# Four rows per ScalarE and VectorE instruction, and a last tile stored in two pieces, in a streaming GELU-gate kernel

## The chip, the cores and the metric

The kernel runs on one core of one Trainium2 chip. The metric is the device time of an execution in microseconds (us), lower is better. The profile is one execution taken by the hardware profiler; its span is about 1.8 us shorter than the device time. Engines: ACT is ScalarE, DVE is VectorE, SP is SyncE (here it only issues DMAs); 16 DMA engines move data between HBM (the chip's large memory) and SBUF (the core's own memory).

## The reference, cut to what matters

```python
x = randn(32, 512, 2048)                      # float32
x1, x2 = x[..., :1024], x[..., 1024:]
out = 0.5 * x1 * (1 + erf(x1 / sqrt(2))) * x2 # float32, (32, 512, 1024)
```

134.22 MB are read and 67.11 MB written. There is no reuse.

## The kernel before

There are 16384 rows of 2048 numbers. A tile holds 8 rows in each of the 128 partitions, so there are 16 tiles: 8.4 MB to load and 4.2 MB to store for each. Two input buffers and two output buffers rotate.

```python
xpool = ctx.enter_context(tc.tile_pool(name="xpool", bufs=2))
opool = ctx.enter_context(tc.tile_pool(name="opool", bufs=2))
# load(i): one dma_start on the SP queue, 8.4 MB
ahead = [load(0), load(1)]
for i in range(n_tiles):
    x_tile = ahead.pop(0)
    o_tile = opool.tile([P, R, half], out.dtype, name="o_tile")
    last = i == n_tiles - 1
    pieces = 4 if last else 1
    step = R // pieces
    for k in range(pieces):
        for r in range(k * step, (k + 1) * step):
            nc.scalar.activation(
                out=x_tile[:, r, :half], in_=x_tile[:, r, :half], func=GELU)
            nc.vector.tensor_mul(
                out=o_tile[:, r, :], in0=x_tile[:, r, :half], in1=x_tile[:, r, half:])
        rows = slice(k * step, (k + 1) * step)
        queue = nc.sync if i >= n_tiles - 2 else nc.scalar
        queue.dma_start(out=o_t[i][:, rows, :], in_=o_tile[:, rows, :])
    if i + 2 < n_tiles:
        ahead.append(load(i + 2))
# ... (cut: flattening, launch)
```

Stores of tiles 0 to 13 go on ACT's queue. The last two go on SP's queue, so tile 14's store stands in line behind the last load there.

Of the kernel before, what the change touches and what calls it, by code (L numbers as in the profile page):

```python
# [1 line left out]

# [4 lines left out]

GELU = mybir.ActivationFunctionType.Gelu


@with_exitstack
def kernel(
    ctx: ExitStack,
    tc: tile.TileContext,
    x: bass.AP,
    out: bass.AP,
):





    nc = tc.nc
    P = nc.NUM_PARTITIONS

    x_flat = x.flatten_outer_dims()
    out_flat = out.flatten_outer_dims()
    n_rows, dim = x_flat.shape
    half = dim // 2

    R = 8
    x_t = x_flat.rearrange("(n p r) d -> n p r d", p=P, r=R)
    o_t = out_flat.rearrange("(n p r) d -> n p r d", p=P, r=R)
    n_tiles = x_t.shape[0]

    xpool = ctx.enter_context(tc.tile_pool(name="xpool", bufs=2))
    opool = ctx.enter_context(tc.tile_pool(name="opool", bufs=2))

    def load(i):
        x_tile = xpool.tile([P, R, dim], x.dtype, name="x_tile")  # L40
        nc.sync.dma_start(out=x_tile, in_=x_t[i])  # L41
        return x_tile

    ahead = [load(0), load(1)]
    for i in range(n_tiles):
        x_tile = ahead.pop(0)
        o_tile = opool.tile([P, R, half], out.dtype, name="o_tile")
        last = i == n_tiles - 1
        pieces = 4 if last else 1
        step = R // pieces  # L50
        for k in range(pieces):
            for r in range(k * step, (k + 1) * step):
                nc.scalar.activation(  # L53
                    out=x_tile[:, r, :half], in_=x_tile[:, r, :half], func=GELU
                )
                nc.vector.tensor_mul(  # L56
                    out=o_tile[:, r, :],
                    in0=x_tile[:, r, :half],
                    in1=x_tile[:, r, half:],
                )  # L60
            rows = slice(k * step, (k + 1) * step)
            queue = nc.sync if i >= n_tiles - 2 else nc.scalar
            queue.dma_start(out=o_t[i][:, rows, :], in_=o_tile[:, rows, :])
        if i + 2 < n_tiles:
            ahead.append(load(i + 2))


# [1 line left out]
_INS = ['x']  # L69
_OUTS = [((32, 512, 1024), 'float32')]  # L70


# [23 lines left out]
```

## Time and profile before

The median was 472.28 us (472.03 to 472.85, 3 runs). What matters:

| reading | value | view |
|---|---|---|
| DMA while in steady state | 433 to 434 GB/s | windows |
| ACT busy, DVE busy | 26%, 31% | page |
| a tile lands every | 29.0 us | landings in the trace |
| compute of a tile, landing to last product | 10.3 us | timeline |
| last load lands | 450.05 us | chain of waits |
| span | 470.5 us | page |

These are lines of the page of the kernel before: busy time of the engines, DMA in 40 slices of the span (9 means 90% or more), the queue of kind "instruction", the chain that ended last, and the two costly groups (line, engine, operation, tiles, shapes, count, then busy us and mean ns of one, then idle time before them).

```profile
DVE 146.7 (31%) x128; ACT 124.2 (26%) x129; POOL 0.2 (0%) x4
...
DMA  8999999999999999999999999999999999999987
...
q14 instruction: 2, 0.02, 0.0%
HBM read 134.22 MB, written 67.11 MB: 428 GB/s over the span
...
DMA x_tile<-in_x_dram 80%; DVE o_tile L56 15%; ACT x_tile L53 2%; DVEq L91 0%; SPq L41 0%; ACTq L53 0%
...
L56 DVE TENSOR_TENSOR o_tile<-x_tile 128x1024 f32<-128x1024 f32 x128 | 146.7, 1218 | 313.7 <-ACT x_tile L53 313.7
L53 ACT ACTIVATE x_tile<-x_tile 128x1024 f32<-128x1024 f32 x128 | 122.9, 1042 | 332.9 <-DMA x_tile<-in_x_dram 332.9
```

The DMA row is full from end to end; both compute engines mostly wait. The chain gives DVE 15%, but that isn't 15% to gain: it follows one of two buffers, and while that buffer is computed on, the other buffer's load is moving.

This is the chain of waits of the kernel before in order of time (start us, length us, what).

```profile
115.36 47.63 DMA x_tile<-in_x_dram
...
173.36 48.46 DMA x_tile<-in_x_dram
...
232.20 47.59 DMA x_tile<-in_x_dram
...
406.07 43.98 DMA x_tile<-in_x_dram
450.05 0.02 issue
...
450.14 1.07 ACT x_tile L53
...
451.23 6.90 DVE o_tile L56 x6
```

### The profile page before, as it was taken

Reading aid. Unit: us, or ns where it says so; the run is one execution under the profiler, and the core shown is the slowest. Engines: PE = TensorE matmul, PEld = TensorE weight load, DVE = VectorE, ACT = ScalarE, POOL = GpSimd, SP = SyncE. Lnnn points to the kernel's source line nnn. Section 1 sums busy time; section 2 is a strip of 40 time slices with the busy share of each in tenths; the row PEclk is TensorE's granted clock in tenths of the full one; section 3 lists DMA queues with packets and bytes.
Section 4 is the critical chain, followed back from the end, with each engine's and each line's share of the span. In section 5 each row is a group of like instructions: output and inputs, shape, how many; then the busy total and the mean of one; then the engine's idle time right before and its main releaser. Section 6 shows DMA issues by size and latency. Waiting matters only on the chain.

```text
span 470.5 us, 408 instructions
## 1 busy us (share of the span) xinstructions
DVE 146.7 (31%) x128; ACT 124.2 (26%) x129; POOL 0.2 (0%) x4
## 2 busy tenths in 40 slices
DVE  0070704307052070520705216061150702507061
ACT  1050605105060150601506024060230603306060
POOL 0000000000000000000000000000000000000000
DMA  8999999999999999999999999999999999999987
GB/s 357 446 446 373 457 423 418 468 429 418 418 446 429 446 407 469 424 429 412 460 432 435 426 443 429 415 437 457 418 443 418 454 440 423 423 449 412 471 382 337
DMA packets 5042, 201.35 MB, mean 428 GB/s; under 512 B 560, under 2 KB 560, under 8 KB 560
## 3 DMA queue, kind: packets, MB, share of 16 engines
q1 hardware_dynamic: 3024, 142.61, 70.4%
q10 hardware_dynamic: 2016, 58.72, 28.9%
q14 instruction: 2, 0.02, 0.0%
HBM read 134.22 MB, written 67.11 MB: 428 GB/s over the span
## 4 chain that ended last, share of the span: by engine, by line
DMA 80%; DVE 15%; ACT 2%; DVEq 0%; issue 0%; SPq 0%; ACTq 0%
DMA x_tile<-in_x_dram 80%; DVE o_tile L56 15%; ACT x_tile L53 2%; DVEq L91 0%; SPq L41 0%; ACTq L53 0%
## 5 line engine op out<-in xcount | busy, mean ns | idle before, releaser
L56 DVE TENSOR_TENSOR o_tile<-x_tile 128x1024 f32<-128x1024 f32 x128 | 146.7, 1218 | 313.7 <-ACT x_tile L53 313.7
L53 ACT ACTIVATE x_tile<-x_tile 128x1024 f32<-128x1024 f32 x128 | 122.9, 1042 | 332.9 <-DMA x_tile<-in_x_dram 332.9
L53 ACT ACT_TABLE_LOAD x1 | 1.3, 1283 | 0.7 <-PEq L80 0.7
L80 POOL MEMSET const-uint8-127<- 128x1 uint8 x1 | 0.1, 102 | 0.0
L80 POOL MEMSET const-bfloat16-1.0<- 128x1 bf16 x1 | 0.1, 101 | 0.0
L80 POOL MEMSET const-float32-0.0<- 128x1 f32 x1 | 0.1, 98 | 0.2 <-issue 0.2
L80 POOL MEMSET const-float32-1.0<- 128x1 f32 x1 | 0.1, 98 | 0.0
## 6 DMA issues: line engine op xcount, KB each, us to landing
out_dram<-o_tile ACTq DMA_DIRECT2D x14, 4096.0 KB, 37.9
out_dram<-o_tile SPq DMA_DIRECT2D x1, 4096.0 KB, 24.7
out_dram<-o_tile SPq DMA_DIRECT2D x4, 1024.0 KB, 8.9
x_tile<-in_x_dram SPq DMA_DIRECT2D x16, 47.6
```

The source lines that it names most:

```text
L53: nc.scalar.activation(out=x_tile[:, r, :half], in_=x_tile[:, r, :half], func=GELU)
L56: nc.vector.tensor_mul(out=o_tile[:, r, :], in0=x_tile[:, r, :half], in1=x_tile[:, r, half:],)
L80: nc = _bacc.Bacc("TRN2", target_bir_lowering=False, num_devices=1)
```

## The change

The intent: fewer, larger instructions, so that their fixed cost is paid a quarter as often (128 products and 128 GELUs become 32 and 32). The last tile has two steps, and each is stored when done.

```diff
-    R = 8
+    R, STEP = 8, 4
...
-        pieces = 4 if last else 1
-        step = R // pieces
-        for k in range(pieces):
-            for r in range(k * step, (k + 1) * step):
-                nc.scalar.activation(
-                    out=x_tile[:, r, :half], in_=x_tile[:, r, :half], func=GELU
-                )
-                nc.vector.tensor_mul(
-                    out=o_tile[:, r, :],
-                    in0=x_tile[:, r, :half],
-                    in1=x_tile[:, r, half:],
-                )
-            rows = slice(k * step, (k + 1) * step)
-            queue = nc.sync if i >= n_tiles - 2 else nc.scalar
-            queue.dma_start(out=o_t[i][:, rows, :], in_=o_tile[:, rows, :])
+        for r in range(0, R, STEP):
+            rows = slice(r, r + STEP)
+            nc.scalar.activation(
+                out=x_tile[:, rows, :half], in_=x_tile[:, rows, :half], func=GELU
+            )
+            nc.vector.tensor_mul(
+                out=o_tile[:, rows, :],
+                in0=x_tile[:, rows, :half],
+                in1=x_tile[:, rows, half:],
+            )
+            if last:
+                store(nc.sync, i, o_tile, rows)
+        if not last:
+            store(nc.sync if i == n_tiles - 2 else nc.scalar, i, o_tile, slice(0, R))
```

More of the change, by code (lines that the diff above doesn't have):

```diff
@@ L42, in load, with store @@
         return x_tile
+    def store(queue, i, o_tile, rows):
+        queue.dma_start(out=o_t[i][:, rows, :], in_=o_tile[:, rows, :])
     ahead = [load(0), load(1)]
```

## The prediction

> **What bounds the kernel now.** The 16 DMA engines. The page has DVE 31% and ACT 26% busy, DMA digits of 9 from end to end, 201.35 MB moved. The windows view reads 433 to 434 GB/s in each 58 us stretch between 106 and 396 us; the DMA packets in the trace keep a share of 1.0 until about 468 us. DVE and ACT only wait (waits view: ACT 332.9 us for loads, DVE 313.7 us for ACT). The Trainium skill ("SBUF — State Buffer", the DMA setup-cost knee) gives 436 GB/s as the port-side asymptote of 16 DMA engines; this trace agrees with 433.
>
> The chain of waits says "DMA 80%, DVE 15%", alternating a load of 47.6 us with 10.26 us of compute. That 15% is misleading: one buffer's load waits for DVE to free it, but the other buffer's load is then in flight. A tile lands every 29.0 us, so the next load is issued 10.3 us into a 29 us stretch in which the queue still has work. About 18 us of slack.
>
> **What the change does.** Elements and bytes stay the same. One row: ACT lasts 1.040 us, pitch 0.949; DVE lasts 1.217, pitch 1.136 (timeline: 7.68 and 9.17 us for eight). With 1024 elements at the slopes these imply (about 0.833 ns and 1.042 ns an element), the fixed cost is about 96 ns of pitch on ACT and 69 ns on DVE. The Trainium skill ("Perfetto Trace Analysis", Optimizing Scalar/DVE Operations) states about 93 and 60 ns; agrees. Estimates for four rows: ACT lasts 3.60 (pitch 3.51), DVE lasts 4.42 (pitch 4.34). Busy: DVE 146.7 -> about 140, ACT 124.2 -> about 115. None of that saving is on the critical path.
>
> Coarser pieces cost latency: DVE now starts after 3.60 us of ACT instead of 1.04. From landing to the last product: 3.60 + 0.03 + 4.34 + 4.42 = 12.4 us against 10.3: +2.1 us a tile. In the 15 first tiles slack absorbs it: each load is issued 2.1 us later and lands at the same time (issue to landing 47.6 -> about 45.5 us). The chain will show about DMA 76, DVE 14, ACT 6%, over the same span.
>
> **Only the end counts.** The last load lands at 450.05 us. Tile 14's store, queued behind it, keeps the DMA engines full until 458.0 to 458.5 us. Before, the first quarter of the last store is issued at 453.6 us, so no gap: data flow until 468.3 us, the last piece lands at 469.5 and the span ends at 470.5. After, the first half is issued at about 450.14 + 3.60 + 0.03 + 4.42 + 0.1 = 458.3 us, just when the engines run dry. With about 1 us from issue to first packet (first load: issued 0.73, first packets after 1.5) the engines idle about 1 us. The second half is issued 4.34 us later, less than the 4.84 us that 2.1 MB take at 433 GB/s, so no second gap. Larger packets (the 8 KB ones run at 428 GB/s) return 0.1 us. Net +0.9 us: predicted 473.2 us, 472.1 to 474.8.
>
> **What would show it.** Right: loads land every 29.0 us; 433 GB/s in the middle; DVE near 140 us; last load landing within 0.5 us of 450; a dip of DMA share near 458 to 460 us; last data near 469. Wrong: a middle period other than 29.0 us; no dip; last load landing elsewhere.
>
> **What would make it wrong.** A larger start delay for a store on an empty ring (2 us would give +1.9); loads and stores interleaving differently once issued 2 us later; four-row instructions costing more than the sum of rows because of their jump between rows; chip-to-chip differences. A change over 2% (9.4 us) would need the middle to lose its overlap, 0.6 us per tile.

## The result, and the profile after

The changed kernel took 471.48 us (471.29 to 472.08, 6 runs), the kernel before 472.22 us (472.03 to 472.85, 6 runs). The ratio is 0.9985, with a 95% interval of 0.9972 to 0.9998. Ratios here are the mean time of one kernel's runs over that of the other's of the same rounds, so not quite the ratio of the medians quoted. By the rule of 2% this is the same time. I had said 472.1 to 474.8 us: a little slower. It was a little faster, outside the range.

The lines of the page after that answer to those of before:

```profile
DVE 140.2 (30%) x32; ACT 115.2 (25%) x33; POOL 0.2 (0%) x4
...
DMA  8999999999999999999999999999999999999988
...
q14 instruction: 2, 0.02, 0.0%
HBM read 134.22 MB, written 67.11 MB: 429 GB/s over the span
...
DMA x_tile<-in_x_dram 77%; DVE o_tile L57 14%; ACT x_tile L54 6%; DVEq L93 1%; SPq L41 0%; ACTq L54 0%
...
L57 DVE TENSOR_TENSOR o_tile<-x_tile 128x4096 f32<-128x4096 f32 x32 | 140.2, 4422 | 321.6 <-ACT x_tile L54 321.6
L54 ACT ACTIVATE x_tile<-x_tile 128x4096 f32<-128x4096 f32 x32 | 114.0, 3608 | 340.5 <-DMA x_tile<-in_x_dram 340.5
```

And the chain of waits after, around the same places:

```profile
114.92 45.50 DMA x_tile<-in_x_dram
...
172.94 45.40 DMA x_tile<-in_x_dram
...
230.87 45.51 DMA x_tile<-in_x_dram
...
405.29 44.00 DMA x_tile<-in_x_dram
449.29 0.02 issue
...
449.37 3.62 ACT x_tile L54
...
453.02 4.43 DVE o_tile L57
457.45 4.33 DVEq L93
```

The sizes of the instructions came out as estimated (4.42 and 3.61 us, busy 140.2 and 115.2), and so did the trade in the middle: compute takes 12.4 us instead of 10.3, the load after it lands 45.5 us after its issue instead of 47.6, the sum is the same. Two things differ from the forecast. No load of this stretch took 0.85 us longer, and the last load lands at 449.29 us, 0.76 us earlier than before. And from that landing to the end of the span it takes 20.44 us, against 20.41 before: the new end costs nothing.

### Where the 0.76 us are: one DMA engine of 16

A load counts as landed when each of the 16 DMA engines has reported its part. The trace has all 16 reports. I compare the last of them with their median: "lateness". The table also has the times at which the trace shows 8 KB packets on queue 14, the one of kind "instruction", after the start. These numbers are worked out from the trace's DMA records.

```
                       before           after
instruction packets    177.8, 196.3     396.4, 453.3
lateness, load landing near
   163 / 160 us        0.43             0.41
   192 / 190           0.54             0.49
   222 / 218           1.22             0.34
   422 / 422           1.08 (at 424.7)  0.92
   last load           1.09             0.49
last load: median      448.97           448.80
last load: last        450.05           449.29
```

In the kernel before, lateness jumps from 0.43 to 1.22 us at the very load that was moving when the second packet came (196.34 us), the load of 48.46 us in the chain. On that DMA engine the packet itself took 0.309 us, and the 64 KB data packet after it took 2.954 us where its like took 2.418: 0.309 + 0.536 = 0.85 us. Every tensor DMA here gives each engine the same share of the bytes, so a late engine stays late until the end, and every load waits for it. This can be checked: in the packet records each packet starts where the one before it on its engine ended, so every engine can be followed and its "lag" taken, the time by which it has moved a given number of bytes, less that of the median engine. The engine that met the second packet was 0.24 us behind before it and 1.09 us behind after it, and so it stayed until the last load was in. (Lateness also depends on the order of load and store packets; lag doesn't. In the kernel after, the packet at 396.4 us met an engine that was 0.12 us ahead and left it 0.39 us behind, while the lateness of the next load is 0.92.) Of the 0.76 us between the two last landings, 0.16 are in the median and 0.60 in the lateness.

By that reading the change gained because it has fewer instructions: the ScalarE and VectorE streams reach the place where more instructions are fetched much later (396 and 453 us), so no fetch holds up an engine for most of the run. The second packet still comes, but at 453.3 us, after the last load.

**Theory (fetch):** an instruction packet delays one DMA engine by 0.5 to 1 us for the rest of the run; the gain is a later or absent packet. **Rival (latency):** the gain comes from the larger instructions or from issuing stores and loads 2 us later. For the end there are two models as well: **mine of the prediction** (the engines of the median run dry at 458.3 us, and every delay past that costs its length) and the **straggler model** (what counts is the slowest engine, which drains last and so finds the next store ready).

### The profile page after: what moved, and what is told of

Same layout as the page of the kernel before. It is cut to its first block, busy times and chain, and to the rows that moved or that the text cites. A ratio compares the mean times of both kernels' runs of the same rounds, so it can differ in the third digit from the quotient of the medians.

```text
span 469.7 us, 213 instructions
## 1 busy us (share of the span) xinstructions
DVE 140.2 (30%) x32; ACT 115.2 (25%) x33; POOL 0.2 (0%) x4
## 4 chain that ended last, share of the span: by engine, by line
DMA 77%; DVE 14%; ACT 6%; DVEq 1%; issue 0%; SPq 0%; ACTq 0%
DMA x_tile<-in_x_dram 77%; DVE o_tile L57 14%; ACT x_tile L54 6%; DVEq L93 1%; SPq L41 0%; ACTq L54 0%
## 5 line engine op out<-in xcount | busy, mean ns | idle before, releaser
L57 DVE TENSOR_TENSOR o_tile<-x_tile 128x4096 f32<-128x4096 f32 x32 | 140.2, 4422 | 321.6 <-ACT x_tile L54 321.6
L54 ACT ACTIVATE x_tile<-x_tile 128x4096 f32<-128x4096 f32 x32 | 114.0, 3608 | 340.5 <-DMA x_tile<-in_x_dram 340.5
## 6 DMA issues: line engine op xcount, KB each, us to landing
x_tile<-in_x_dram SPq DMA_DIRECT2D x16, 45.5
```

The source lines that it names most:

```text
L54: nc.scalar.activation(out=x_tile[:, rows, :half], in_=x_tile[:, rows, :half], func=GELU)
L57: nc.vector.tensor_mul(out=o_tile[:, rows, :], in0=x_tile[:, rows, :half], in1=x_tile[:, rows, half:],)
```

## The experiments

All results in one table. Medians of the runs; "before" is the kernel before in the same rounds; "gap" is the idle time that each of the 16 DMA engines has between tile 14's store and the last tile's store (least / median / most, from the DMA packets; blank where it wasn't worked out). e9_fewer_pad, e5_dve96, e8_last2222 and e3_before2 ran on another chip than the rest.

```
run             median  (low - high)       before   ratio   instr. packets  last load lands (lateness)  gap
control_after   471.58  (471.50-472.32)    472.26   0.9990  396.3, 453.3    449.26 (0.50)    0.00/0.19/0.60
e1_pad          471.87  (471.63-471.97)    472.26   0.9990  178.8, 196.8    449.89 (1.03)    0.00/0.67/1.14
e2_fewer        471.21  (471.18-471.32)    472.26   0.9978  470.4           449.23 (0.31)    0.00/0.03/0.26
e4_last53       473.30  (473.11-473.68)    472.26   1.0022  396.3, 453.2    449.29 (0.43)    1.48/2.07/2.35
e9_fewer_pad    471.47  (471.30-471.73)    472.14   0.9986  179.8, 194.5    449.43 (0.52)
e5_dve96        481.75  (481.66-482.56)    472.14   1.0207  13 packets      458.91 (10.01)
e8_last2222     471.60  (471.52-471.84)    472.14   0.9989  396.5, 453.1    449.41 (0.69)    0.00/0.00/0.01
e3_before2      471.85  (471.69-472.08)    472.14   0.9994  180.1, 198.3    449.72 (0.93)    0.00/0.00/0.00
e11_busy        471.96  (471.72-472.37)    471.88   1.0003  193.6, 400.1    450.22 (1.31)
e7_last8        478.87  (478.74-478.99)    471.88   1.0148  396.3, 453.2    449.27 (0.52)    7.24/7.90/8.25
before_again    472.25  (472.00-472.33)    471.88   1.0007  180.2, 198.4    450.07 (1.05)
e1_pad_again    472.04  (471.62-473.40)    471.88   1.0007  178.7, 193.5    449.98 (1.20)    0.00/0.85/1.16
```

All outputs are right. Read the small differences with care: before_again is the same program as "before" and differs from it by 0.37 us in the median. So a few tenths of a microsecond in the time prove nothing alone; the landings in the trace are the finer instrument.

### Control: the changed kernel again

No edit. 

> The changed kernel once more, as the control of this group. Both theories: about 471.5 us, 0.7 us under the kernel before. Fetch theory (the 8 KB packets of the instruction queue delay one of 16 DMA engines, which cannot catch up since each engine owns a fixed share of the bytes): two such packets, near 396 and 453 us; the 16 engines' parts of a load land within 0.7 us of one another until 396 us; the last load lands at about 449.3 us.

It came nearly as written: 471.58 us, packets at 396.3 and 453.3 us, last load at 449.26 us, lateness 0.32 to 0.47 us until 392 us. The first and last part of a load were up to 0.76 us apart there, where I had said 0.7.

### e1_pad, e1_pad_again: as many instructions as before, but four-row work

```diff
...  # cut: the declaration of the one-element tiles pad_a and pad_d
+        if not last:
+            for _ in range(6):
+                nc.scalar.activation(out=pad_a, in_=x_tile[:, 0, :1], func=GELU)
+            for _ in range(6):
+                nc.vector.tensor_copy(out=pad_d, in_=o_tile[:, 7, :1])
```

> The changed kernel with 6 one-element instructions more per tile on each of ScalarE and VectorE, so that the instruction count is that of the kernel before, while the four-row work, its latency of 12.4 us per tile and the two-piece end stay. Fetch theory: the two instruction packets move back to about 175 to 205 us, after which one engine's part of each load lands 0.6 to 1.1 us after the median; the last load lands between 449.6 and 450.1 us; time 471.9 to 472.4 us. Rival (the gain comes from issuing stores and loads 2 us later, or from large instructions): last load at 449.3 us, time 471.5 us as the control.

The packets moved back as forecast, to 178.8 and 196.8 us, and the last load landed at 449.89 us. But this profile doesn't show the fetch as the cause: one engine was late from the start (lateness 1.13 us at the second load, 45 us into the run, before any packet), and the packets hit other engines. The median of 471.87 us misses my range by 0.03, and the mean of the runs equals that of the control. So I ran it again.

> e1_pad once more (its first profile had an engine late from the start of the run, which hid what the instruction packets did): packets near 179 and 197 us; without a late start, last landing minus median is about 0.4 us until 160 us and 0.7 to 1.1 us from about 215 us on; time 471.9 us, 0.3 us over the changed kernel. Rival: 471.5 us.

This time no engine was late at the start, and the effect stands free. Lateness of its loads, in order: 0.36, 0.42, 0.56, 0.41, 0.45, 0.35, 0.50, then from the load across 193.5 us on 1.18, 1.18, 1.28, 1.32, 1.35, 1.32, 1.41, 1.39, 1.20. The last load landed at 449.98 us, 0.72 later than in the control, with the medians of the 16 reports 0.03 us apart (448.785 and 448.758). The four-row instructions and the 2.1 us of extra compute latency were there all the same; the rival would have left the landing at 449.3. But not all of the 0.72 us is the fetch's. The engine's lag rose from 0.05 to 0.89 us at the packet of 193.5 us, and then to 1.22 by two slow data packets (2.67 us at 248.7 us and 2.49 at 307.0, for 2.42) with no instruction packet before them. Without those two, by my estimate, the last load would have landed 0.4 us later than in the control. The span grew from 469.73 to 470.20 us (0.46 from the unrounded spans) and not by 0.72, because the end took up the rest; see the gaps below.

### e2_fewer, e9_fewer_pad: still fewer instructions, and the count restored

```diff
-        for r in range(0, R, STEP):
-            rows = slice(r, r + STEP)
+        steps = [4, 4] if last else [8]
+        for k, step in enumerate(steps):
+            r = sum(steps[:k])
+            rows = slice(r, r + step)
...  # each GELU is kept behind the store of the tile before in ACT's issue order
```

> One eight-row instruction per tile and engine for tiles 0 to 14 (compute 15.9 us per tile instead of 12.4), two four-row ones for the last tile as in the changed kernel. Fetch theory: the engines never get to the instruction that starts a fetch before the end, so none or only a very late instruction packet; spread last minus median of each load about 0.4 us to the end; last load lands at about 449.0 us; time 471.0 to 471.4 us. Rival (latency itself gains): 3.5 us more latency gain again as much as 2.1 us did, or about 470.4 us. If the slack of 29 us per tile is not real, the time grows by up to 3.5 us a tile.

No instruction packet came before 470.4 us, when all data had moved. Lateness stayed between 0.19 and 0.36 us to the end. All five runs lie within 0.14 us of one another (471.18 to 471.32), below all five of the control. This kernel is a little faster than both the one before (ratio 0.9978, interval 0.9965 to 0.9992) and the changed one (471.58 us in the same rounds), though by the rule of 2% all three are the same. Compute latency rose by 3.5 us a tile with no loss: the slack of the middle is real. The last load, though, landed at 449.23 us, not at 449.0, and about where the control's did; the gain shows at the end, where the last data packet ended at 468.26 us against 468.52 in the control, in which the packet at 453.3 us made one engine end 0.24 us after the next. The profile's page of this run has no queue 14:

```profile
q1 hardware_dynamic: 2736, 142.61, 70.5%
q10 hardware_dynamic: 2016, 58.72, 29.0%
```

e9_fewer_pad adds 7 one-element instructions per tile and engine to it.

> The kernel with one eight-row instruction per tile (e2_fewer), with 7 one-element instructions more per tile on each of ScalarE and VectorE, so that the count of instructions is about that of the kernel before. Fetch theory: two 8 KB instruction packets in the middle, near 170 to 210 us, each holding one DMA engine up by 0.55 to 0.85 us; last landing minus median rises from 0.3 us to 0.6 to 1.1 us in the loads after them; time about 471.6 to 472.0 us, 0.4 to 0.8 over e2_fewer, and more spread between runs. Rival (the gain of e2_fewer comes from latency or size of instructions, not from the fetches): 471.2 us as e2_fewer.

The packets came at 179.8 and 194.5 us, and lateness rose from 0.25 to 0.54 and 0.91 us at the loads across them. Then it shrank, to 0.52 at the last load, since the other engines lost a little too (from 217 us on a load took 29.04 us by the median report and 28.99 by the last). The time was 0.26 us over e2_fewer's: the sign was right, the size below my 0.4 to 0.8, and 0.13 under my lower bound of the time. The two ran on different chips and in different rounds, so the 0.26 is weak evidence; the lateness is the better.

### e5_dve96, e11_busy: many fetches, and the same busy time without them

```diff
...  # cut: the tiles pad_a and pad_d, and a loop for ScalarE that runs 0 times
+        if not last:
+            for _ in range(96):
+                nc.vector.tensor_copy(out=pad_d, in_=o_tile[:, 7, :1])
```

> The changed kernel with 96 one-element VectorE instructions more per tile, in VectorE's idle time after its products: about 1,500 instructions instead of 68. Fetch theory: about 12 instruction packets of VectorE. If all use the same DMA engine, that engine is late by 12 x 0.55 to 0.85 us, 6.6 to 10 us, and so is every load and the time: 478 to 481 us. If they go around the 16 engines, lateness hardly adds up: 471.9 to 472.7 us. Rival (fetches cost nothing): 471.5 us.

The time went to 481.75 us, a little past the upper guess (ratio 1.0207, interval 1.0193 to 1.0221). The trace has 13 instruction packets; all but the one at 407.2 us (66 ScalarE instructions had started there) keep step with VectorE's long stream, one in about 128 of its instructions. Lateness climbs from load to load, in steps of about 0.9 us a packet: 0.46, 0.77, 1.60, 2.57, 3.54, 4.52, 4.31, 5.27, 6.24, 7.18, 7.19, 8.16, 9.13, 10.02, 10.01. At the last load the median report came at 448.90 us, as in every other run; the 15th came at 450.56 and the 16th at 458.91. So the fetches of VectorE's stream all fell on one DMA engine, and fifteen engines waited for it for 8 to 10 us. The page and the windows view (window, length, busy us of DVE, ACT and POOL with counts, TensorE clock, mean DMA share, GB/s) of this run:

```profile
q14 instruction: 13, 0.11, 0.1%
...
L74 DVE COPY pad_d<-o_tile 128x1 f32<-128x1 f32 x1440 | 220.9, 153 | 49.7
```

```profile
396.00:450.00 54.00, 42.17 (x165) 14.25 (x4) 0.00 (x0) 1.00 1.00 434
450.00:459.00 9.00, 7.34 (x49) 0.00 (x1) 0.00 (x0) 1.00 0.86 371
459.00:469.00 10.00, 8.57 (x17) 7.12 (x2) 0.00 (x0) 1.00 0.18 75
469.00:479.00 10.00, 2.40 (x1) 0.00 (x0) 0.00 (x0) 1.00 0.87 369
```

The mean share is full until 450 us, falls to 0.18 for ten microseconds and comes back for the last store. VectorE is also much busier here, which a rival could blame. Hence the control with six long products in place of the 96 short copies:

```diff
...  # cut: the declaration of pad_d, here of 2 x 1024 elements
+        if not last:
+            for _ in range(6):
+                nc.vector.tensor_mul(
+                    out=pad_d.rearrange("p (r d) -> p r d", d=half),
+                    in0=o_tile[:, 6:, :],
+                    in1=o_tile[:, 6:, :],
+                )
```

> Control of e5_dve96: the changed kernel with VectorE kept busy equally long after each tile (6 products of 128x2048, about 13.7 us a tile, against 14.7 us for 96 one-element copies), but with only 90 instructions more. Fetch theory: one or two instruction packets of VectorE instead of eleven, last load's last landing within 1.2 us of its median, time 471.5 to 472.3 us. Rival (VectorE's busy time, which holds up the next tile's products, made e5_dve96 slow): near 481 us.

It took 471.96 us. Its VectorE padding took about as long in all (the groups view):

```profile
L71 DVE TENSOR_TENSOR pad_d<-o_tile 128x2048 f32<-128x2048 f32 x90 | 206.3, 2292 | 3.1
```

So busy time isn't what slowed e5_dve96. Here one packet fell at 193.6 us, and lateness went from 0.40 to 1.22 us there and stayed (my bound of 1.2 at the last load was passed by 0.1). The second, at 400.1 us, met another engine and did not raise it further.

### e8_last2222, e3_before2, e4_last53, e7_last8: the end

```diff
 e8: steps of the last tile [4, 4] -> [2, 2, 2, 2]      (rest as changed)
 e3: pieces = 4 if last else 1 -> pieces = 2 if last else 1   (rest as before)
 e4: steps of the last tile [4, 4] -> [5, 3]            (rest as changed)
 e7: steps of the last tile [4, 4] -> [8]               (rest as changed)
```

> The changed kernel with the last tile cut into four pieces of two rows for computing and storing, the rest as changed: the end takes its first store about 3.7 us earlier. Model of the prediction (the two-piece end costs 0.9 us of idle engines): 470.6 us. Straggler model (the slowest engine gets its piece before it has drained tile 14's store, so nothing is lost by two pieces): equal to the control within 0.25 us, 471.3 to 471.6 us, although no engine idles at 458 us any more.

471.60 us against 471.58: four pieces gain nothing over two (on another chip, with "before" 0.12 us lower there), though the idle gap is gone from all 16 engines. My prediction had put 0.9 us on this.

> The kernel before with the last tile's store in two pieces instead of four, one-row instructions kept. Both models: the first half is ready at about 456.6 us after a landing at 450.0, before any engine runs dry, so nothing changes: 472.2 us, within 0.25. If four small pieces cost or gain something of their own, it shows here.

471.85 us, 0.29 below its "before", just outside the quarter microsecond that I allowed, and within what two series of the same program differ by. There may be a small real part: from the last landing to the end it took 20.24 us against 20.41. An estimate from the packets: half of the last store is 256 packets of 8 KB at 309 ns before and 128 of 16 KB at 611 ns here, 0.06 us less per engine, 0.11 for the whole store.

> The changed kernel with the last tile cut 5 rows and 3 rows instead of 4 and 4. Straggler model of the end: from the last load's last packet, the slowest engine needs 9.70 us for its share of tile 14's store; landing, 5 rows of ScalarE (4.45), 5 rows of VectorE (5.49), issue and start come to about 11.2 us, so it idles 1.5 us: time 1.5 us over the control (473.0 us). Model of the prediction (engines of the median run dry at 458.3 us, every later start costs its whole delay): the two-piece end already costs 0.9 us, and one row more adds the 2.0 us that one row takes on both engines: 473.5 us.

473.30 us, 1.72 over the control (span: 1.64). The expectations were 1.5 and 2.0 over it; the least gap of an engine is 1.48 us, the median 2.07. This lies between, nearer the straggler model, because a gap of this size makes all engines start the last store together and end together (470.07 to 470.23 us).

> The changed kernel with the last tile as one piece of eight rows. Straggler model of the end: from the last packet of the last load to the first packet of the store 0.33 + 7.02 + 0.03 + 8.69 + 0.1 + 0.85 = 17.0 us, against 9.70 us of store of tile 14 to drain: 7.3 us of idle DMA, all of it on the critical path: 478.9 us. If a coarser end were harmless in general: 471.5 us.

478.87 us; the straggler model said 478.9. The least gap is 7.24 us, for a forecast of 7.3. The windows view of this run shows the hole:

```profile
450.00:458.00 8.00, 1.59 (x1) 6.38 (x1) 0.00 (x0) 1.00 0.92 398
458.00:459.00 1.00, 1.00 (x1) 0.00 (x0) 0.00 (x0) 1.00 0.01 0
459.00:466.00 7.00, 6.10 (x1) 0.00 (x0) 0.00 (x0) 1.00 0.08 33
466.00:476.00 10.00, 0.00 (x0) 0.00 (x0) 0.00 (x0) 1.00 0.93 396
```

Why a half-tile end is free and a whole-tile end is not is one sum. When the slowest engine has moved its last load packet, it still has eight store packets of tile 14, 8 x 1.213 = 9.70 us. In that time the load must report (0.33 us; 0.29 to 0.41 in these traces), four rows must pass ScalarE and VectorE and the store be issued (457.48 - 449.29 = 8.19 us), and its first packet must start (0.85 us after the issue): 9.37 us. That leaves about a third of a microsecond. The faster engines do idle, 0.19 us in the control and 0.85 us in the median of e1_pad_again, but they idle only because they are ahead, and in e1_pad_again the late engine still ends last (469.07 us, median 468.84). By this sum, a start that comes later by more than about 0.3 us costs what it exceeds that.

### before_again

> The kernel before, profiled once more, to see whether its late engine is a habit: two instruction packets near 178 and 196 us again; last landing minus median rises at the load across 196 us and the last load lands 0.9 us or more after its median; time 472.2 us, equal to itself within 0.3 us, which is the noise of this comparison.

Packets at 180.2 and 198.4 us, last load at 450.07 us with a lateness of 1.05; the time is 0.37 us from that of the same program, where I had allowed 0.3. The jump that I expected can't be read from the reports: from the second load on the last report of each load is 1.9 us after the median, down to 1.05 at the last load. e3_before2 is the same, 2.2 and then 0.93. My reading, not tested: some engines had put a load packet (2.42 us) behind store packets and kept that order, which moves their reports without making them late in work. The lag shows the jump, and more: the engine that met the packet at 198.4 us went from 0.06 us ahead of the median to 0.68 us behind, but the engine that finished the last load latest was another, 0.64 us behind at 48 us already and 0.87 at the end. In e3_before2 the latest engine had been 1.00 us behind at 48 us, and the packets left theirs 0.4 and 0.8 us behind. So in these two runs, as in e1_pad, a packet delayed an engine, but an early straggler, whose cause no run here shows, set the last landing.

## Why the prediction was wrong

- **The engines' sums: right.** ACT lasts 3.61 (said 3.60), DVE 4.42 (4.42), busy 115.2 (about 115) and 140.2 (about 140). The slopes per element that I used can't be read from one size alone; the two sizes give (3608 - 1040) / 3072 = 0.836 ns on ACT and (4422 - 1217) / 3072 = 1.043 ns on DVE, close to my 0.833 and 1.042. The fixed cost that the change saves is off the critical path, as said.
- **The middle: right.** Tiles land every 29 us, loads take 45.5 us instead of 47.6, DMA at 434 GB/s. e2_fewer added 3.5 us more of latency without harm.
- **"The last load lands at 450.05 us" and stays within 0.5 us: wrong.** It landed at 449.29. I read the tail's landings off one run and took them for a property of the byte count. They hold 1.09 us of lateness of a single engine, most of it since the instruction packet at 196.3 us. With fewer instructions the packet came later and on e2_fewer practically not at all. Restoring the count of instructions alone brought the landing back to 449.98 us (e1_pad_again), where by my estimate 0.4 of the 0.72 us over the control are the fetch's.
- **"Data flow until 458.0 to 458.5 ... so the engines idle about 1 us ... net +0.9 us": wrong in its cost.** Its size was right where the landing is late: the median engine of e1_pad_again idled 0.85 us. But I used the time at which the median engine runs dry, with a landing that is set by the slowest. The slowest engine has 9.70 us of work for a wait of about 9.4, so the term is 0. Measured: 20.44 us from last landing to end, 20.41 before; e8_last2222 equals the control within 0.02 us.

The forecast of +0.9 thus was 0 and -0.76 in the two profiles: -0.73 together in the span (470.46 to 469.73 us). How the -0.76 divides is shown better in the trace than in the time. In e1_pad_again the landing came 0.72 us and the end of the span 0.46 us after the control's; by the estimate above about 0.4 us of that landing is the fetch's. In the medians, restoring the count cost 0.26 us (e9_fewer_pad over e2_fewer) and 0.29 us (e1_pad over the control of its rounds; their means are equal), and a comparison of a program with itself strayed by 0.37. So that fetches delay an engine by 0.5 to 1 us is shown, and that in the profile before such an engine set the last landing; that they make up all of the 0.7 us is not. What stays open is a remainder of some 0.3 to 0.5 us: 0.16 us in the median landing, the larger packets of the last store (0.1 by the estimate above), and engines that are late from the start or meet slow data packets, as in e1_pad, e1_pad_again and before_again.

## What to carry to other kernels

In this kernel, bound by DMA, saving instruction time gained nothing in itself, and coarser instructions were free as long as their latency fitted the slack. In another such kernel, find out where it doesn't (here the last tile, with about 0.3 us to spare), and keep the pieces small there alone. A transfer is done when its slowest DMA engine is, so look at the last of the 16 reports, not at the mean share: one disturbed engine delayed everything in e5_dve96, and a mean of 1.0 hid it. Very many tiny instructions on an engine with idle time are not free (1440 of them cost some 10 us there), since their fetches go through the same DMA engines. And follow the late engine back to where it became late before you name a cause: the profile before and before_again end with about the same lateness (1.09 and 1.05 us) and had got it in different ways.

## What the Trainium skill lacked or had wrong

- DMA: Bandwidth & Descriptors, "Queues, rings and completion order", names row 14 as runtime-internal; it doesn't say that instruction fetches there hold up tensor traffic. Runtime: NRT & Kernel Launch, "Instruction fetch mechanics", where the point belongs too, doesn't give that cost either. In these runs an 8 KB packet of queue 14 took 0.309 to 0.316 us amid tensor traffic, and with the stretched 64 KB packet behind it cost one engine 0.55 to 0.98 us for good (0.309 + 0.244 to 0.316 + 0.661). VectorE's eleven until the last load of e5_dve96 brought its lateness from 0.4 to 10.0 us. The first came when 57 to 75 instructions of a stream had started (sequencer's instructions counted), VectorE's later ones in e5_dve96 every 111 to 153, about 128 in the mean ((1356 - 75) / 10).
- SBUF — State Buffer (its table of bandwidths) and DMA: Bandwidth & Descriptors (Specifications) put HBM at about 358 GB/s per core, below the 435 of the fabric, and the summary of rules of the SBUF page gives 358 without a condition as the figure for HBM transfers. This one core moved 433 to 434 GB/s between HBM and SBUF in every steady window; the 436 GB/s of "the DMA setup-cost knee" is what fits. The DMA page's own section "Measured" has the condition that the rule lacks: about 358 is each core's part when both cores of an HBM domain stream. No run here has two cores.
- No page that I found says that a coarse end is judged by the slowest engine. Perfetto Trace Analysis, "Identifying Performance Opportunities", warns that the 16 engines make occupancy misleading; e5_dve96 shows by how much: share 1.00 in the mean, one engine 10 us late.
- Right, with a number: VectorE: DVE Perf Modes, in its section on SBUF-source operations, gives (N + 151) / 0.96 ns for a float32 two-tensor operation, by which an estimate for 4096 elements is 4424 ns; measured 4422.
